# Input casts and side work behind each product's evictions, and another order of the last steps, in a four-layer decoder step

## The chip, the cores and the metric

The kernel runs on one core of one Trainium2 chip. What counts is the time of one execution in microseconds (us). A core has a tensor engine for matmuls (PE; its weight loads are PEld), a vector engine (VectorE, in the profile DVE), a scalar engine (ScalarE, ACT), GpSimd (POOL) and a sync engine (SyncE, SP). SP here does little but start transfers (DMAs) between the memory outside the core and its on-chip buffer. Matmul results land in PSUM, a small memory in banks. ACT and DVE take them out of there, which is called an eviction below. Each engine works through its own list of instructions in order. One that has to wait holds up everything behind it in its list.

## The reference

One step of a decoder: 1,024 prompt positions and 8 single decode positions, width 2,048. There is one pooling layer, then one shared projection to keys and values, then one attention layer with a window of 128. Each layer has an input product, a gate, an output product and a layer norm.

```python
def pool_layer(x, prefix, pos, w_in, w_grp, scale, w_out, g_ln, b_ln):
    z = x @ w_in
    u, gate = z[..., :D_POOL], z[..., D_POOL:]
    d, new_state = multiscale_pool(u, prefix, pos)
    d = jnp.einsum('btgc,gce->btge', d.reshape(B, T, N_POOL_GROUPS, POOL_GROUP), w_grp)
    y = (d.reshape(B, T, D_POOL) * scale * jax.nn.silu(gate)) @ w_out
    return layer_norm(ALPHA * x + y, g_ln, b_ln), new_state

def attn_layer(x, ..., w_in, sinks, w_out, g_ln, b_ln):
    z = x @ w_in
    q = rope_partial(z[..., :D_ATTN].reshape(B, T, N_HEADS, HEAD_DIM), pos)
    gate = z[..., D_ATTN:]
    o = attn_core(q, kb, vb, q_pos, k_pos, sinks).reshape(B, T, D_ATTN)
    y = (o * jax.nn.silu(gate)) @ w_out
    return layer_norm(ALPHA * x + y, g_ln, b_ln)
```

All of it is in fp32.

## The kernel before

**Tiling.** The positions are worked in two chunks of 512 and 520 columns (the second holds the 8 decode positions). Every layer has two phases, its input product (`ai`, `bi`) and its output product (`ao`, `bo`), each over both chunks. A phase computes pairs of output tiles with a Strassen scheme: `seven` makes seven products in place of eight (`ORDER7` is their order: 0, 2, 1, 5, 3, 4, 6). Each product's operands are sums or differences of quarter matrices, and its result is added into the PSUM banks a, b and c in turn (`names`).

**Precision.** A matmul of fp32 is done as three matmuls of rounded operands. Every weight tile and every input tile is split into a rounded high part, which ACT makes by a cast (`cast_to`, L491, for weights; `x_cast`, L796, for inputs), and a residual, which DVE makes by a subtraction (L506 in `prep_to` for weights, L805 in `x_make` for inputs). One product is 8 times the three matmuls L661, L662 and L663.

**A product's steps.** `begin` first calls `flush`, which runs the list `posts`, the evictions of the product before. Then it asks for loads and prepares weights three to seven products ahead. Then `run` issues the 24 matmuls and puts this product's own eviction in `posts`, and `end` follows. The evictions are p0 (L609, ACT), p2 (L615, ACT), p1 (L618, ACT), p5 (L624, ACT), p3 (L629, DVE), p4 (L634, DVE) and p6 (L641, ACT). Since the banks go round, one product later PE wants the bank back that an eviction is reading.

**What stands in `end`.** Sums of weights that come late, products from other work (`self.pe`), the `events` due at this product, and then two things in which the change lies. `x_tick` (L812) looks whether an input tile of the next phase may be loaded, cast (L796) or given its residual (L805); each depends on the free buffers and the tile's age. Below it the side work, generators that make sums of weights (L439 to L444) or a layer norm of the chunk before (L932 to L934, L1005), takes a step if enough buffers are free. `in_order` at the end of the program pins the lists of PE, DVE and ACT to the order in which the source issues them, so nothing is moved later.

**The end.** `phase_end` closes the last layer for the second chunk. `TAIL` is an order of the last products in which three pairs of tiles (x, y, z) are interleaved, and `steps` says which small work goes with which product. Behind the last product the layer norm needs the moments of two halves of the columns (A and Bh). `affine1` (two DVE operations, L1423 and L1424) and `affine2` (two ACT operations, L1431, and a store) scale a pair of tiles. Most rows leave the core transposed: `turn` transposes on PE (L1531), `last_rows` adds a rank-one term (L1540), `factors` transposes the row factors (L1519), `evict` takes 512 columns out of PSUM, on ACT (L1554) or DVE (L1552), and starts a 512 KB store to `y1b` (second half) or `y1a` (first half) for every two. `last_four` (L1565 to L1568 and a store) writes the few columns that are left. `moments` is a chain that goes between ACT and DVE (L1500 to L1512, L1497).

## Time and profile before

| | before |
|---|---|
| runs, us | 2304.54, 2304.70, 2308.23 |
| median, us | 2304.7 |
| the profiled execution, us | 2305.89 |
| its span in the trace, us | 2304.1 |
| granted TensorE clock, mean | 0.999 |
| instructions | 50417 |
| bytes moved by DMA, MB | 654.58 |

The span runs from the first to the last instruction or transfer in the trace; the execution's own time is 1.79 us more. In the rows below, a row of the timeline gives start, duration, engine, line, operation, shapes, and in brackets the idle time ahead of it and what ended it. A row of the windows gives a stretch of time and, for each engine, its busy us and its instructions, then the granted clock, the share of the DMA engines that was busy and GB/s. A matmul of this kernel is started every 0.12 us though each lasts 0.28 us, since matmuls overlap; PE's idle time is therefore read from the brackets.

### The profile page before, as it was taken

The numbers are of one execution on the slowest core, as the hardware profiler recorded it, in microseconds if no ns is written. First come the engines' busy times: TensorE is split into PE (matmuls) and PEld (weight loads), VectorE is DVE, ScalarE is ACT, GpSimd is POOL, SyncE is SP. The second block draws the span as 40 slices with busy tenths as digits, with TensorE's granted clock in tenths as the row PEclk, the third lists the DMA queues.
The fourth block names the chain that finished last, engine by engine and source line by source line (L and its number), as shares of the span: only waits on it lengthen the run. The fifth ranks groups of instructions, "written<-read, shape, count | busy, mean of one in ns | idle before, by whom it ended". The sixth has DMA issues, their size and how long they took to land. (4 is left out here: it accounts for less than half of the span.)

```text
span 2304.1 us, 50417 instructions
## 1 busy us (share of the span) xinstructions
PE 2283.5 (99%) x20279; PEld 2209.6 (96%) x20279; DVE 1902.1 (83%) x2433; ACT 1368.2 (59%) x2533; POOL 198.1 (9%) x400
## 2 busy tenths in 40 slices
PE   9999999999999999999999999999999999999998
PEld 7899999999999999999889999999999999999998
DVE  8787889777878878988888888899776777888896
ACT  4444446544546546555466776785776678656565
POOL 0111110011010000000011111100000000010001
PEclk9999999999999999999999999999999999999999
DMA  8768789988989988999687667787686678799794
GB/s 292 243 233 296 262 298 364 328 306 289 309 306 313 350 286 305 338 389 351 230 305 255 230 231 248 256 291 233 223 255 229 218 225 306 250 364 383 254 347 172
DMA packets 248220, 654.58 MB, mean 284 GB/s; under 512 B 26385, under 2 KB 106033, under 8 KB 247985
## 3 DMA queue, kind: packets, MB, share of 16 engines
q1 hardware_dynamic: 204816, 494.67, 63.8%
q0 software_dynamic: 43168, 156.68, 17.6%
q8 instruction: 159, 2.61, 0.5%
q14 instruction: 77, 0.62, 0.1%
HBM read 464.54 MB, written 177.20 MB: 279 GB/s over the span
## 5 line engine op out<-in xcount | busy, mean ns | idle before, releaser
L661 PE MATMUL pD<-m,m 128*128 128x260 f32 (+1 forms) x4976 | 1409.1, 283 | 6.8 <-DVE m L629 3.0
L662 PE MATMUL pD<-m,m 128*128 128x260 f32 (+1 forms) x4976 | 1401.8, 282 | 0.0
L663 PE MATMUL pD<-m,m 128*128 128x260 f32 (+1 forms) x4976 | 1401.2, 282 | 0.6 <-DVE m L506 0.5
L661 PEld LDWEIGHTS pD<-m,m 128*128 128x128 f32 x4976 | 936.8, 188 | 12.1 <-issue 2.3
L663 PEld LDWEIGHTS pD<-m,m 128*128 128x128 f32 x4976 | 937.3, 188 | 1.1 <-DVE m L506 1.1
L662 PEld LDWEIGHTS pD<-m,m 128*128 128x128 f32 x4976 | 936.8, 188 | 0.5
L506 DVE TENSOR_TENSOR m<-m,m 128x1024 fp32r<-128x1024 f32 x684 | 827.6, 1218 | 76.7 <-ACT m L491 42.9
L491 ACT CAST m<-m 128x1024 fp32r<-128x1024 f32 x684 | 712.8, 1048 | 286.8 <-DVE m L343 86.4
L343 DVE TENSOR_TENSOR m<-m,m 128x1024 f32<-128x1024 f32 x120 | 146.6, 1222 | 10.2 <-DMA m<-in_wia 6.9
L805 DVE TENSOR_TENSOR m<-m,m 128x1024 fp32r<-128x1024 f32 (+1 forms) x118 | 144.2, 1225 | 5.9 <-ACT m L796 3.2
L641 ACT COPY m<-pD 128x260 f32<-128x260 f32 (+1 forms) x87 | 32.5, 374 | 188.5 <-PE pD L663 188.5
L796 ACT CAST m<-m 128x1024 fp32r<-128x1024 f32 (+1 forms) x118 | 123.8, 1054 | 4.4 <-DMA m<-in_x 2.4
L689 PE MATMUL pD<-m,m 128*128 128x512 f32 x288 | 114.3, 397 | 0.0
L691 PE MATMUL pD<-m,m 128*128 128x512 f32 x288 | 113.5, 394 | 0.0
L690 PE MATMUL pD<-m,m 128*128 128x512 f32 x288 | 113.2, 393 | 0.0
L629 DVE TENSOR_TENSOR m<-pD,m 128x260 f32<-128x260 f32 (+1 forms) x90 | 38.1, 423 | 74.9 <-PE pD L663 74.9
L1870 ACT ACTIVATE m<-m,sm 128x128 f32<-128x128 f32 x256 | 99.3, 390 | 0.0
L1892 ACT ACTIVATE m<-m,sm 128x128 f32<-128x128 f32 (+1 forms) x320 | 93.8, 373 | 0.0
L1133 PE MATMUL pD<-m,m 128*128 128x260 f32 (+1 forms) x528 | 91.4, 323 | 0.0
L1133 PEld LDWEIGHTS pD<-m,m 128*128 128x128 f32 x528 | 79.4, 188 | 8.2
L618 ACT COPY m<-pD 128x260 f32<-128x260 f32 (+1 forms) x90 | 33.6, 374 | 90.3 <-PE pD L663 90.2
L609 ACT ACTIVATE pD<-pD 128x260 f32<-128x260 f32 (+1 forms) x88 | 32.5, 369 | 78.2 <-PE pD L663 68.2
(257 smaller groups left out, 2187.4 us busy)
## 6 DMA issues: line engine op xcount, KB each, us to landing
m<-in_wib SPq DMA_DIRECT2D x132, 512.0 KB
m<-in_wia SPq DMA_DIRECT2D x122, 512.0 KB
swia<-m POOLq DMA_DIRECT2D x64, 512.0 KB, 5.0
m<-swia SPq DMA_DIRECT2D x64, 512.0 KB
m<-swoa SPq DMA_DIRECT2D x64, 512.0 KB
m<-swob SPq DMA_DIRECT2D x56, 512.0 KB
m<-in_wob SPq DMA_DIRECT2D x52, 512.0 KB
m<-in_woa SPq DMA_DIRECT2D x48, 512.0 KB
```

Of the source, the lines that this page charges most:

```text
L343: self.nc.vector.tensor_add(s[out].a[:, :1024], s[x].a[:, :1024], s[y].a[:, :1024])
L491: self.nc.scalar.copy(hi.r[:, :1024], self.stream[self.cast].src().a[:, :1024])
L506: self.nc.vector.tensor_sub(lo.r[:, :1024], s.src().a[:, :1024], hi.a[:, :1024])
L661: nc.tensor.matmul(ps[:, :TH], wh[:, s], h, start=new and k == 0, stop=False, skip_group_check=on)
L662: nc.tensor.matmul(ps[:, :TH], wh[:, s], l, start=False, stop=False, skip_group_check=on)
L663: nc.tensor.matmul(ps[:, :TH], wl[:, s], h, start=False, stop=k == 7, skip_group_check=on)
L689: nc.tensor.matmul(ps[:], wh[:, s], h, start=par == 0 and k == 0, stop=False)
L690: nc.tensor.matmul(ps[:], wh[:, s], l, start=False, stop=False)
L691: nc.tensor.matmul(ps[:], wl[:, s], h, start=False, stop=par == 1 and k == 7)
L796: self.nc.scalar.copy(h.r[:, :n], s.a[:, :n])
L805: self.nc.vector.tensor_sub(l.r[:, :n], s.a[:, :n], h.a[:, :n])
L1133: nc.tensor.matmul(ps[:, : cs.stop - cs.start], ws[:, s], d[:, cs], start=f0 and k == 0, stop=l0 and k == 3,)
```

## The change

`end` no longer runs `x_tick` and the side work. It appends both to a new list, `owed`, and `flush` empties that list behind the evictions, at the next `begin` (and in the plain products `unit` and `two_units` also halfway). In the last steps, `affine1(4, Bh)` moves into the step of the product (z, 6); `affine2` can be done by halves, and the half of z goes into `moments` as `early`; a third eviction of the second half goes into `between`, ahead of the cast L1512; `last_four` for the first half stands ahead of the first half's evictions; and the factors and the first `last_rows` stand ahead of transposes.

```diff
--- before.py
+++ after.py
@@ -204,7 +204,7 @@
         self.mem = Mem(pool("mem", bufs=1), NSLOT)
         self.n = 0
         self.i = self.e = self.lastO = self.turns = self.ring = 0
-        self.posts, self.events, self.side = [], {}, []
+        self.posts, self.events, self.side, self.owed = [], {}, [], []
         self.extra, self.on = None, False
         self.fresh = None
         self.ahead = 7, 4, 3
@@ -514,6 +514,8 @@
         todo, self.posts = self.posts, []
         for go in todo:
             go()
+        while self.owed:
+            self.owed.pop(0)()
 
     def begin(self):
         self.flush()
@@ -540,7 +542,9 @@
         for go in self.events.pop(self.i, []):
             go()
         self.i += 1
-        self.x_tick()
+        self.owed += [self.x_tick, self.work]
+
+    def work(self):
         room = len(self.mem.whole()) - 2 * len(self.xq)
         if self.extra and next(self.extra, 1):
             self.extra = None
@@ -1423,13 +1427,14 @@
             nc.vector.tensor_sub(t, t, b2(box["m", h.start]))
             nc.vector.tensor_mul(t, t, b2(box["r", h.start]))
 
-        def affine2(p, h):
+        def affine2(p, h, js=(0, 1)):
             t = tv(p)[:, :, h]
-            for j in range(2):
+            for j in js:
                 m = 2 * p + j
                 g, b = (self.prm[:, i + m : i + m + 1] for i in (gc, bc))
                 nc.scalar.activation(t[:, j], t[:, j], AF.Identity, bias=b, scale=g)
-            nc.sync.dma_start(out[:, 2 * p : 2 * p + 2, :], t)
+            if 1 in js:
+                nc.sync.dma_start(out[:, 2 * p : 2 * p + 2, :], t)
 
         def back(p):
             pre[p] = self.mem.full()
@@ -1486,7 +1491,7 @@
                         skip_group_check=True,
                     )
 
-        def moments(at=0, between=lambda: None):
+        def moments(at=0, between=lambda: None, early=lambda: None):
 
             mb, vb = R[at]
             w, h, S = self.mem.full(), self.mem.full(), [self.mem.half() for _ in range(4)]
@@ -1502,6 +1507,7 @@
             nc.vector.scalar_tensor_tensor(v, vb[:, :TH], EPS, qq, op0=ALU.add, op1=ALU.subtract)
             nc.scalar.mul(X[hi], m[hi, A2], -1.0)
             nc.scalar.copy(M[hi], X[hi])
+            early()
             nc.scalar.activation(r, v, AF.Abs_reciprocal_sqrt)
             back32(32)
             nc.vector.tensor_mul(qq, r, r)
@@ -1606,7 +1612,7 @@
             (z, 5): [
                 lambda: square(y, A), lambda: factors2(TH), lambda: spare(4), lambda: scale(4),
             ],
-            (z, 6): [lambda: add(y, A), lambda: spare(y), lambda: scale(y)],
+            (z, 6): [lambda: add(y, A), lambda: affine1(4, Bh), lambda: spare(y), lambda: scale(y)],
         }
         for p, idx in TAIL:
             for go in steps.get((p, idx), []):
@@ -1643,31 +1649,31 @@
         turn(0, 0, 0, 8)
 
         def between():
-            for b in range(2):
-                evict(B, b, 0)
-
-        moments(0, between)
-        for b in range(2):
-            evict(B, b, 1, "DVE")
-        affine2(z, Bh)
+            evict(B, 0, 0)
+            evict(B, 1, 0)
+            evict(B, 0, 1, "DVE")
+
+        moments(0, between, lambda: affine2(z, Bh, (0,)))
+        evict(B, 1, 1, "DVE")
+        last_four(0, f3, NK, io["y1c"])
         X[0, 0, 2], X[0, 0, 3] = self.psW(), self.psW()
         turn(0, 0, 8, 16)
+        factors(0)
+        factors2(0)
         X[0, 1, 0], X[0, 1, 1] = self.psD(), self.psD()
-        turn(0, 1, 0, 8)
+        turn(0, 1, 0, 4)
+        last_rows(0, 0, range(4))
+        turn(0, 1, 4, 8)
         X[0, 1, 2] = self.psO()
         turn(0, 1, 8, 12)
-        factors(0)
-        factors2(0)
-        affine1(4, Bh)
-        last_rows(0, 0, range(4))
         last_rows(0, 1, range(3))
         for k in range(4):
             evict(0, 0, k)
         X[0, 1, 3] = self.psD()
         turn(0, 1, 12, 16)
         last_rows(0, 1, (3,))
+        affine2(z, Bh, (1,))
         affine2(4, Bh)
-        last_four(0, f3, NK, io["y1c"])
         for k in range(4):
             evict(0, 1, k)
```

The lists of the engines change as follows; the letters m, pD, pO stand for buffers (m on chip, pD and pO in PSUM), and the numbers in them differ between the two kernels. L809, L633, L1291, L1334 and L1560 of the changed kernel are the lines L805, L629, L1287, L1330 and L1554 of the kernel before; L506 keeps its number. L343 sums quarters of a weight, L272 is the residual of a pooled tile, L1287 adds the layer's input to a finished pair of tiles, and L1330 begins the sums of its layer norm.

The first place is DVE's list in the first layer's input product, some 344 us into the program, before the change:

```order
L343 TENSOR_TENSOR m_427_3646<-m_426_3644,m_427_3646 128x1024
L805 TENSOR_TENSOR m_438_3748<-m_416_3593,m_433_3712 128x1040
L629 TENSOR_TENSOR m_434_3714<-pD_3597,m_425_3642 128x256
L506 TENSOR_TENSOR m_440_3753<-m_418_3599,m_437_3720 128x1024
L343 TENSOR_TENSOR m_426_3644<-m_418_3599,m_426_3644 128x1024
```
After:

```order
L343 TENSOR_TENSOR m_427_3646<-m_426_3644,m_427_3646 128x1024
L633 TENSOR_TENSOR m_433_3712<-pD_3597,m_425_3642 128x256
L809 TENSOR_TENSOR m_438_3749<-m_413_3562,m_434_3714 128x1040
L506 TENSOR_TENSOR m_440_3753<-m_420_3603,m_437_3720 128x1024
L343 TENSOR_TENSOR m_426_3644<-m_420_3603,m_426_3644 128x1024
```

Ten rows behind these, still in DVE's list, before:

```order
L506 TENSOR_TENSOR m_447_3828<-m_418_3599,m_445_3794 128x1024
L272 TENSOR_TENSOR m_449_3857<-m_443_3788,m_449_3857 128x512
L805 TENSOR_TENSOR m_450_3860<-m_417_3595,m_439_3750 128x1040
L506 TENSOR_TENSOR m_455_3872<-m_435_3716,m_448_3830 128x1024
L343 TENSOR_TENSOR m_435_3716<-m_435_3716,m_418_3599 128x1024
L805 TENSOR_TENSOR m_457_3903<-m_423_3638,m_451_3862 128x1040
L506 TENSOR_TENSOR m_463_3915<-m_426_3644,m_456_3874 128x1024
```
The same stretch of DVE's list after:

```order
L809 TENSOR_TENSOR m_446_3826<-m_414_3564,m_439_3751 128x1040
L506 TENSOR_TENSOR m_449_3832<-m_420_3603,m_445_3794 128x1024
L272 TENSOR_TENSOR m_451_3861<-m_443_3788,m_451_3861 128x512
L809 TENSOR_TENSOR m_452_3866<-m_418_3599,m_447_3828 128x1040
L506 TENSOR_TENSOR m_457_3876<-m_435_3716,m_450_3834 128x1024
L343 TENSOR_TENSOR m_435_3716<-m_435_3716,m_420_3603 128x1024
L809 TENSOR_TENSOR m_460_3909<-m_419_3601,m_453_3868 128x1040
```

The eviction p3 (the row that reads a pD) has moved ahead of the input residual. Further on, an input residual (L805, now L809) stands ahead of each of three weight residuals (L506) that it stood behind.

The second place is DVE's list in the output product of the same layer, some 910 us in, around the addition L1287 that a pair's evictions end with. Before:

```order
L506 TENSOR_TENSOR m_1273_10787<-m_1250_10640,m_1268_10752 128x1024
L805 TENSOR_TENSOR m_1275_10815<-m_1248_10635,m_1270_10780 128x1040
L1287 SCALAR_TENSOR_TENSOR m_1259_10709<-m_1234_10551,m_1259_10709 128x1024
L506 TENSOR_TENSOR m_1281_10828<-m_1255_10676,m_1274_10789 128x1024
L1330 TENSOR_TENSOR m_1259_10709<-m_1259_10709,m_1111_9436 128x1024
L805 TENSOR_TENSOR m_1283_10859<-m_1249_10637,m_1276_10817 128x1040
L506 TENSOR_TENSOR m_1287_10870<-m_1260_10711,m_1282_10830 128x1024
L805 TENSOR_TENSOR m_1290_10901<-m_1254_10673,m_1284_10861 128x1040
```
After:

```order
L809 TENSOR_TENSOR m_1272_10785<-m_1244_10602,m_1267_10750 128x1040
L506 TENSOR_TENSOR m_1276_10793<-m_1252_10644,m_1271_10758 128x1024
L1291 SCALAR_TENSOR_TENSOR m_1259_10709<-m_1234_10551,m_1259_10709 128x1024
L809 TENSOR_TENSOR m_1278_10823<-m_1250_10640,m_1273_10787 128x1040
L506 TENSOR_TENSOR m_1284_10834<-m_1256_10678,m_1277_10795 128x1024
L1334 TENSOR_TENSOR m_1259_10709<-m_1259_10709,m_1110_9429 128x1024
L809 TENSOR_TENSOR m_1286_10868<-m_1251_10642,m_1279_10825 128x1040
L506 TENSOR_TENSOR m_1290_10876<-m_1263_10717,m_1285_10836 128x1024
L809 TENSOR_TENSOR m_1293_10910<-m_1262_10715,m_1287_10870 128x1040
```

Ahead of L1287 the same number of input residuals has been made in both. Behind it, an input residual now comes first, and each weight residual that follows has one input residual more ahead of it than before.

The third place is ACT's list at the end, from the copy that opens `moments` on. Before:

```order
L1500 COPY m_3008_28269<-pD_28428 128x260
L1503 ACTIVATE m_3013_28488<-m_3008_28269 64x256
L1504 CAST m_3014_28489<-m_3013_28488 64x256
L1505 ACTIVATE m_3016_28491<-m_3015_28490 128x260
L1554 ACTIVATE m_3017_28500<-pD_28454,m_2863_26945 128x512
L1554 ACTIVATE m_3018_28502<-pO_28456,m_2863_26945 128x512
L1512 CAST m_3014_28489<-m_3013_28488 64x256
L1554 ACTIVATE m_3017_28500<-pD_28455,m_2863_26945 128x512
L1554 ACTIVATE m_3018_28502<-pD_28457,m_2863_26945 128x512
L1431 ACTIVATE m_2973_27959<-m_2973_27959,prm 128x260 x2
L1526 COPY m_2863_26945<-pD_28541 128x2
```
After (L1505, L1508, L1509, L1511 and L1518 are L1500, L1503, L1504, L1505 and L1512 of before, and L1435 is L1431):

```order
L1505 COPY m_3009_28270<-pD_28431 128x260
L1508 ACTIVATE m_3014_28491<-m_3009_28270 64x256
L1509 CAST m_3015_28492<-m_3014_28491 64x256
L1435 ACTIVATE m_2973_27946<-m_2973_27946,prm 128x260
L1511 ACTIVATE m_3017_28494<-m_3016_28493 128x260
L1560 ACTIVATE m_3018_28504<-pD_28457,m_2864_26946 128x512
L1560 ACTIVATE m_3019_28506<-pO_28459,m_2864_26946 128x512
L1560 ACTIVATE m_3018_28504<-pD_28458,m_2864_26946 128x512
L1518 CAST m_3015_28492<-m_3014_28491 64x256
L1560 ACTIVATE m_3019_28506<-pD_28460,m_2864_26946 128x512
L1532 COPY m_2864_26946<-pD_28532 128x2
```

One scaling of `affine2` (L1431) has moved ahead of the fourth operation of `moments`, and the third eviction of the second half ahead of the cast L1512; the fourth eviction is behind it as before, and the other scaling has left this stretch.

## The prediction

> **What bounds the kernel now.** The first view is the profile's page, for the busy time of the engines; the second groups PE's idle time by what ended it.
>
> ```profile
> PE 2283.5 (99%) x20279; PEld 2209.6 (96%) x20279; DVE 1902.1 (83%) x2433; ACT 1368.2 (59%) x2533; POOL 198.1 (9%) x400
> ...
> PE pD L661 <- DVE m L629: 3.0, 3, 1.3
> PE pD L661 <- ACT pD L609: 1.7, 2, 1.3
> PE pD L661 <- ACT m L618: 1.5, 1, 1.5
> PE pS L1936 <- DVE m L1903: 1.1, 3, 0.5
> PE pD L663 <- DVE m L506: 0.5, 1, 0.5
> ```
>
> PE is busy for 2283.5 of 2304.1 us, so 20.6 us is all that better order can reach. Work on PE is not changed in number. The rows name who keeps PE waiting: evictions, that is DVE's L629 (3.0 us in 3 waits) and ACT's L609 and L618, and DVE's L1903, a copy of scores. These are the rows that the change can touch; the four hold 7.3 us. For a weight residual, L506, PE waits only once, 0.5 us. The rest is start, end and waits of other kinds. So the forecast is a sum of some ten single waits, and I read each of them in the timeline: does the late eviction stand behind a cast, a residual or side work that the change puts behind it?
>
> **The evictions that come earlier.** Rows of PE give the wait in brackets; rows of DVE and ACT show what the eviction stood behind.
>
> ```profile
> 1237.39 2.35 DVE L805 TENSOR_TENSOR m<-m,m 128x1024 fp32r<-128x1024 f32 x2
> 1240.23 0.36 PE L661 MATMUL pD<-m,m 128*128 128x256 f32 x1 [0.41 <-DVE m L629]
> 1513.71 0.45 PE L1936 MATMUL pS<-m,m 64*64 64x128 f32 x8 [0.26 <-DVE m L1903]
> 1944.98 1.03 ACT L796 CAST m<-m 128x1024 fp32r<-128x1024 f32 x1
> 1945.92 0.36 ACT L609 ACTIVATE pD<-pD 128x256 f32<-128x256 f32 x1
> 1948.01 0.45 PE L1936 MATMUL pS<-m,m 64*64 64x128 f32 x8 [0.49 <-DVE m L1903]
> 2128.76 1.04 ACT L796 CAST m<-m 128x1040 fp32r<-128x1040 f32 x1
> 2130.13 0.39 PE L661 MATMUL pD<-m,m 128*128 128x260 f32 x1 [0.63 <-ACT m L624]
> 2173.68 0.69 DVE L932 TENSOR_TENSOR m<-m 128x512 f32<-128x512 f32 x1 [0.20 <-ACT m L931]
> 2175.74 0.42 DVE L629 TENSOR_TENSOR m<-pD,m 128x260 f32<-128x260 f32 x1
> 2176.31 0.36 PE L661 MATMUL pD<-m,m 128*128 128x260 f32 x1 [1.26 <-DVE m L629]
> ```
>
> In each of the places the row ahead of the eviction is an input residual, an input cast or side work, and lasts longer than PE waits. At 1240, L629 stands behind two residuals of together 2.35 us and PE waits 0.41. At 1948 PE waits for a copy of scores (L1902, which DVE's L1903 reads) that stands behind L609 and the cast L796 of 1.03; the wait at 1513.71 has the same shape. At 2130 it is the cast, 1.04 against a wait of 0.63. At 2176 it is side work: L932 to L934 took from 2173.68 to 2175.74, PE waited 1.26, and in the changed order L629 stands ahead of all three. The sum is 0.41 + 0.26 + 0.49 + 0.63 + 1.26 = **3.05 us**, each term taken whole because the work that is put behind is longer than the wait. What is late next: the cast, the residual or the layer norm that was put behind. A cast or residual is made for a tile that some later product reads, and the layer norm for an output, so a delay of 0.4 us is covered by the products between. If that cover were gone, the term would return as a wait for the moved work, up to the eviction's own 0.36 to 0.42.
>
> **Two stretches in which DVE has no room.** The first is the input product of the first layer.
>
> ```profile
> 344.26 1.22 DVE L343 TENSOR_TENSOR m<-m,m 128x1024 f32<-128x1024 f32 x1 [1.47 <-DMA m<-in_wia]
> 345.40 1.23 DVE L805 TENSOR_TENSOR m<-m,m 128x1040 fp32r<-128x1040 f32 x1
> 346.56 0.42 DVE L629 TENSOR_TENSOR m<-pD,m 128x256 f32<-128x256 f32 x1
> 347.12 0.36 PE L661 MATMUL pD<-m,m 128*128 128x256 f32 x1 [1.29 <-DVE m L629]
> 356.16 1.05 ACT L796 CAST m<-m 128x1040 fp32r<-128x1040 f32 x1
> 357.12 0.36 ACT L609 ACTIVATE pD<-pD 128x256 f32<-128x256 f32 x1
> 357.54 0.38 PE L661 MATMUL pD<-m,m 128*128 128x256 f32 x1 [1.27 <-ACT pD L609]
> ...
> 343.00:372.00 29.00, 26.30 (x217) 25.71 (x217) 27.53 (x31) 18.62 (x24) 2.13 (x4) 1.00 0.91 315
> ```
>
> Taken alone, both waits would nearly go: L629 stands 1.16 behind L805 (345.40 to 346.56), L609 0.96 behind L796, of 1.29 and 1.27 waited, together 2.12 us. But the row of the window gives DVE 27.53 busy of 29.00: it idles 1.47, all of it in the wait for a load at 344.26. The work of DVE in this stretch does not shrink, and by the order some ten rows on one input residual more stands ahead of each of three weight residuals, 1.16 us for one (345.40 to 346.56). So DVE itself allows 1.47 - 1.16 = 0.3 us of gain, and only where the load that it waits for comes earlier by that. The bounds are +2.1 us, where those weight residuals have time to spare, and -1.2 us, where the load comes when it came and PE then waits for a weight residual by the whole step. I take **+0.3 us**, since the window row is nearest to the question.
>
> The second stretch is the output product of that layer.
>
> ```profile
> 912.92 1.23 DVE L1287 SCALAR_TENSOR_TENSOR m<-m,m 128x1024 f32<-128x1024 f32 x1 [1.30 <-ACT m L641]
> ...
> 929.10 0.39 PE L663 MATMUL pD<-m,m 128*128 128x260 f32 x1 [0.51 <-DVE m L506]
> 935.43 0.50 PE L910 MATMUL pO<-m,jr 128*128 128x512 f32 x1 [0.35 <-DVE m L894]
> ...
> 908.00:938.00 30.00, 29.15 (x239) 28.57 (x239) 28.70 (x28) 23.38 (x33) 0.54 (x1) 1.00 0.98 364
> ```
>
> DVE is busy 28.70 of 30.00 and its only pause is the 1.30 ahead of L1287, which waits for the pair's last eviction. Before, a weight residual comes first behind L1287. In the changed order an input residual stands directly behind L1287 and ahead of the weight residuals, so each is late by the step of 1.16 us until the counts are equal again just ahead of L894. PE already waits 0.51 for one of them at 929.10, so that one has no room at all: its wait grows by 1.1 us. L894 is not later, so a PE that comes later no longer waits 0.35 there. Net loss 1.1 - 0.35 = **0.75 us**, with bounds of 0 and 1.2.
>
> **What stays.** The longest wait, 1.52 us for L618 (its row in the groups above), comes from an ACT that a weight cast holds up, and the cast waits for rotary work that counts as an event; events stay ahead of evictions. I put it and the waits of its kind at zero, with 0.5 us either way for chance. The main part then gives 3.05 + 0.3 - 0.75 = **2.6 us**.
>
> **The end.** Behind PE's last matmul the transfers set the end; the row with x24 is a piece of the chain that ended last, the last row one of the windows.
>
> ```profile
> 2283.96 0.43 DVE L639 TENSOR_TENSOR m<-pD,m 128x260 f32<-128x260 f32 x1 [1.23 <-PE pD L663]
> 2284.30 0.69 DVE L1423 TENSOR_TENSOR m<-m,m 128x520 f32<-128x520 f32 x1
> 2284.45 0.59 POOL L1447 COPY m<-m 128x8 f32<-128x8 f32 x1 [3.15 <-DVE m L639]
> 2288.75 0.42 ACT L1505 ACTIVATE m<-m 128x260 f32<-128x260 f32 x1 [0.75 <-DVE m L1502]
> 2290.03 0.68 ACT L1554 ACTIVATE m<-pO,m 128x512 f32<-128x512 f32 x1
> 2291.05 0.40 ACT L1512 CAST m<-m 64x256 fp32r<-64x256 f32 x1 [0.34 <-DVE m L1511]
> 2291.48 1.26 ACT L1554 ACTIVATE m<-pD,m 128x512 f32<-128x512 f32 x2
> 2290.11 2.76 PE pD L1531 x24
> 2292.19 0.92 SPq L1556 DMA_DIRECT2D out_y1b<-m  x2
> 2294.93 0.99 SPq L1556 DMA_DIRECT2D out_y1a<-m  x2
> 2293.00:2302.50 9.50, 2.85 (x17) 2.16 (x15) 3.91 (x9) 4.18 (x9) 0.00 (x0) 0.85 1.01 390
> ```
>
> From 2293.0 to 2302.5 the DMA share is 1.01 at 390 GB/s, 9.5 x 390 = 3.7 MB, which is six stores of 0.52 MB, two of 0.27 (128 x 520 floats) and small ones. So what counts is when the first store starts and whether the queue runs dry. The third eviction, which completes the first store, moves from 2291.48 to directly behind 2290.03 + 0.6: the first store is issued some 0.85 earlier, at 2291.3. But the fourth still needs L1512, so the two y1b stores (2 x 0.52 MB, 2.7 us at 390 GB/s) end near 2294.85, and the stores of y1a must follow. Ahead of the first half's evictions 8 transposes less stand on PE (2.76 us for 24 of them, so 0.9 us for these), but the factors want the bank that the fourth eviction frees, near 2292.3, so I take half, 0.6 earlier than 2294.93, and data some 0.85 behind the issue, as from 2292.19 to where the window of transfers begins: 2295.2. The queue is dry for 0.3. From there 2.63 MB at 390 GB/s take 6.7, to 2301.9 instead of 2302.5: **0.6 us**, bounds 0.2 (the queue runs dry longer) and 0.9 (not at all). The scaling of 0.69 + 0.70 goes into VectorE's pause of 1.23 and makes L639 late by 0.15, which DVE passes to `moments`; ACT's wait of 0.75 ahead of L1505 takes up the scaling that is put there, at half of that wait or all of it, and neither is seen by the first store, which waits for L1554.
>
> L1423 at 2284.30 lasts 0.69 although a copy on POOL runs beside it (2284.45, 0.59): DVE's next instruction was not held up by it. [...]
>
> **The sum.** 2.6 + 0.6 = 3.2 us. From the profiled execution's 2305.89 that gives 2302.7; this execution was 1.2 us above the median of the three runs, so on the median it is 2304.7 - 3.2 = **2301.5 us**.
>
> **The rivals.**
>
> *All of it goes.* The weight residuals have time to spare in both stretches: 3.05 + 2.1 + 0.9 = 6.1 us, with nothing lost, **2298.6 us**. For it: most weight residuals are made three products ahead, and DVE idles 17% over the span. Against it: the two windows, where DVE is 95% busy.
>
> *It is taken up again.* Casts and residuals come later throughout, and another of these tight places takes what an eviction gave; only the end gains: 2304.7 - 0.6 = **2304.1 us**. For it: waits move along a full engine rather than vanish. Against it: in 1200 to 2200 us DVE has pauses ahead of most evictions, where lateness ends.
>
> *Slower.* In the changed order input residuals stand ahead of weight residuals that they stood behind, and PE needs the weight residuals first. Each place where a weight residual has no room costs 1.16 us. I count one such place, behind 912, and half of one behind 344; with three more the kernel would be slower than before, and with eight it would be so by 8 x 1.16 - 3.2 = 6.1 us, **2310.8 us**. For it: L805's work is the same 1.23 us wherever it stands, and the ticks are moved in every phase. Against it: before, PE waits for a weight residual only once, so most have room for a step.
>
> *It doesn't do what it says.* The order shows evictions ahead of the ticks on both engines, so this has no chance left.
>
> **How the numbers follow.** Chances: forecast 0.45, all of it 0.22, taken up again 0.23, slower 0.10. A measurement of this kernel can tell 0.2%, 4.6 us, from no change, so faster means below 2300.1 and slower above 2309.3. All of the second case and a fifth of the first are faster: 0.22 + 0.09 = 0.31. Of the last case 0.08 is slower. The rest, 0.61, is within. The range begins 0.6 below the second case's time, at 2298.0, since the waits held at zero may move by 0.5 too, and ends 1.2 above the third's, for one more tight place, at 2305.3; outside lie the last case and a tenth of the others.
>
> **What would show it.** Right: no waits of PE for L629, L609 or L624 behind a tick at 1240, 2130 and 2176; the waits for L1903 gone at 1513 and 1948; a wait for L506 near 929 of about 1.6; the first y1b store near 2291.3 of the old time scale. Wrong: PE's idle total not below 18, new waits for L506 or L805 in other stretches, loads that come later because buffers come free later, or a hole of over 0.5 us in the transfers of the last ten.

## The result and the profile after

The changed kernel is slower, by 0.8%.

| | before | after |
|---|---|---|
| median of the runs | 2304.7 us | 2323.9 us |
| lowest and highest | 2304.5 to 2308.2 (3 runs shown above) | 2322.5 to 2326.0 (6 runs) |
| ratio, 95% interval | | 1.0079 (1.0069 to 1.0090) |
| profiled execution | 2305.89, span 2304.1 | 2325.30, span 2323.4 |
| PE busy / idle within the span | 2283.5 / 20.6 | 2292.8 / 30.6 |

One more run of the kernel before, taken beside these, lasted 4520.59 us; nothing on record says why, and neither the table nor the ratio counts it.

The forecast was 2301.5, its range 2298.0 to 2305.3: the time lies 22.4 us above the one and 18.6 above the upper end of the other. The span grew by 19.3 us, half of it idle time of PE (+10.0), half busy time of PE (+9.3), although PE does the same work.

In the changed kernel four lines have been added ahead of the matmuls, so L661 is now L665, L663 is L667, the first eviction of a product, L609, is L613, L618 is L622, L629 is L633, L639 is L643, the input cast L796 is L800, the residual L805 is L809, the store L857 is L861, L1903 is L1909. The weight cast and the weight residual keep L491 and L506. The first view is the page of the changed kernel (busy time), the second its list of waits of PE: line that waited, line waited for, us in total, times, longest.

```profile
PE 2292.8 (99%) x20279; PEld 2217.1 (95%) x20279; DVE 1902.3 (82%) x2433; ACT 1367.9 (59%) x2533; POOL 196.6 (8%) x400
...
PE pD L665 <- ACT pD L613: 11.8, 4, 4.9
PE pD L667 <- DVE m L506: 2.6, 6, 0.6
PE pD L665 <- ACT m L622: 2.1, 1, 2.1
PE pD L1525 <- ACT m L1560: 1.5, 1, 1.5
PE pD L2252 <- POOL m L1056: 1.3, 1, 1.3
PE pS L1942 <- DVE m L1909: 1.1, 3, 0.5
```

The row for DVE's L629 (now L633), 3.0 us before, is gone, and so is that for ACT's L624: this is what the change was forecast to do. In its place ACT's L613, the first eviction of a product, has gone from 1.7 us in 2 waits to 11.8 in 4. The four are single rows of PE's timeline:

```profile
356.99 0.38 PE L665 MATMUL pD<-m,m 128*128 128x256 f32 x1 [2.43 <-ACT pD L613]
1064.43 0.39 PE L665 MATMUL pD<-m,m 128*128 128x260 f32 x1 [1.07 <-ACT pD L613]
1284.20 0.39 PE L665 MATMUL pD<-m,m 128*128 128x256 f32 x1 [3.33 <-ACT pD L613]
1502.64 0.58 PE L665 MATMUL pD<-m,m 128*128 128x256 f32 x1 [4.93 <-ACT pD L613]
```

**Why L613 is late.** ACT's timeline ahead of three of these rows:

```profile
355.10 1.04 ACT L491 CAST m<-m 128x1024 fp32r<-128x1024 f32 x1 [2.71 <-DVE m L809]
356.05 0.61 ACT L271 CAST m<-m 128x512 fp32r<-128x512 f32 x1
356.57 0.36 ACT L613 ACTIVATE pD<-pD 128x256 f32<-128x256 f32 x1
...
1281.19 1.04 ACT L491 CAST m<-m 128x1024 fp32r<-128x1024 f32 x1 [4.70 <-DMA to<-m]
1282.14 0.20 ACT L1874 ACTIVATE sm<-sm 128x8 f32<-128x8 f32 x1
...
1283.79 0.36 ACT L613 ACTIVATE pD<-pD 128x256 f32<-128x256 f32 x1
...
1499.62 1.04 ACT L491 CAST m<-m 128x1024 fp32r<-128x1024 f32 x1 [7.17 <-DMA to<-m]
```

The weight cast L491 waits 4.70 and 7.17 us for a DMA named `to<-m`. That is not a load: it is a store, by which a tile leaves for the scratch array `to` in HBM. The cast doesn't read what the store carries. It writes into the buffer that the store is still reading, and begins when the store has landed (the stores at 1281.17 and 1499.46, the casts at 1281.19 and 1499.62). The names in the order of the changed kernel (buffer, then a running number of the allocation) say so, on POOL and on ACT:

```
230 L861 DMA to0_87<-m42_1732_14784 128x1024
...
923 L491 CAST m42_1739_14839<-m20_1726_14661 128x1024
```

Buffer m42 is given to a stored tile as allocation 1732, and the weight cast takes the same buffer as allocation 1739, seven later. At the second place it is m39 (allocations 1952 and 1960). At 355.10 the cast writes the buffer from which DVE's L809 has just read an input tile. In the kernel before, no cast stands so close behind a store: the shortest distances there are 10, to an eviction copy and to a load, and 11, one of them to a weight cast. The chain that ended last runs through both stores (start, duration, line):

```profile
1275.40 5.77 DMA to<-m
...
1490.53 8.93 DMA to<-m
```

So the change put input casts, residuals and side work between the evictions and the weight cast of the next product; these take the buffers that stood free, and the weight cast gets the one that has just been released. (Whether another rule of handing out could have spared these two casts no run shows; `e5_other_buffers`, below, is the nearest.) The eviction L613 stands behind the cast in ACT's list and runs behind it (1283.79 and 1281.19 above), and PE waits for it until 1284.20.

**Why PE is busier.** The windows behind three of the waits (busy time of PE, PEld, DVE, ACT, POOL, then the granted clock, DMA share, GB/s):

```profile
358.00:360.00 2.00, 2.00 (x11) 2.00 (x11) 1.97 (x3) 1.12 (x2) 0.00 (x0) 0.50 1.08 381
1286.00:1289.00 3.00, 3.00 (x16) 3.00 (x16) 2.59 (x4) 2.34 (x8) 0.00 (x0) 0.50 0.46 188
1502.00:1507.00 5.00, 4.36 (x20) 4.37 (x21) 3.44 (x5) 4.30 (x14) 0.53 (x1) 0.50 1.08 327
```

After the long waits, near 1502 already during it, the TensorE clock is granted at 0.50, three times for 3.4 us and once, near 1502, for 6.8, and matmuls follow each other by 0.21 us instead of 0.12. Each matmul of the main stream was compared with its counterpart before: the lag grows behind the four drops (near 357, 1284, 1502 and 1589) by 1.5, 1.6, 2.3 and 1.5 us, which is 6.9 of the 9.3 us of added busy time.

**The account.** The same comparison gives where the lag came and went (us, after minus before, at the program's places): 347 -1.5; 357 to 360 +2.6; 931 to 936 -0.6; 962 to 1005 +2.6; 1060 +1.3; 1240 -0.6; 1272 to 1282 +5.0; 1488 to 1505 +7.8; 1572 to 1580 +2.1; 2130 -0.9; 2169 to 2176 -1.5; 2281 +0.9. The last matmul of the products begins 17.3 us later (2300.98 instead of 2283.64), and from there to the end of the span it takes 22.4 instead of 20.5, another +1.9.

### The profile page after: what moved, and what is told of

It reads as the page before. It is cut to its first block, busy times and chain, and to the rows that moved or that the text cites. A ratio compares the mean times of both kernels' runs of the same rounds, so it can differ in the third digit from the quotient of the medians.

```text
span 2323.4 us, 50388 instructions
## 1 busy us (share of the span) xinstructions
PE 2292.8 (99%) x20279; PEld 2217.1 (95%) x20279; DVE 1902.3 (82%) x2433; ACT 1367.9 (59%) x2533; POOL 196.6 (8%) x400
## 5 line engine op out<-in xcount | busy, mean ns | idle before, releaser
L665 PE MATMUL pD<-m,m 128*128 128x260 f32 (+1 forms) x4976 | 1413.0, 284 | 13.9 <-ACT pD L613 11.8
L667 PE MATMUL pD<-m,m 128*128 128x260 f32 (+1 forms) x4976 | 1405.7, 282 | 2.8 <-DVE m L506 2.6
L665 PEld LDWEIGHTS pD<-m,m 128*128 128x128 f32 x4976 | 940.3, 189 | 19.2 <-ACT pD L613 12.6
L667 PEld LDWEIGHTS pD<-m,m 128*128 128x128 f32 x4976 | 940.9, 189 | 4.5 <-DVE m L506 4.4
L506 DVE TENSOR_TENSOR m<-m,m 128x1024 fp32r<-128x1024 f32 x684 | 828.1, 1219 | 89.1 <-ACT m L491 49.3
L491 ACT CAST m<-m 128x1024 fp32r<-128x1024 f32 x684 | 711.8, 1048 | 306.3 <-DVE m L343 81.2
L343 DVE TENSOR_TENSOR m<-m,m 128x1024 f32<-128x1024 f32 x120 | 146.6, 1222 | 7.6 <-DMA m<-in_wia 4.0
L809 DVE TENSOR_TENSOR m<-m,m 128x1024 fp32r<-128x1024 f32 (+1 forms) x118 | 144.3, 1226 | 8.5 <-ACT m L800 4.4
L800 ACT CAST m<-m 128x1024 fp32r<-128x1024 f32 (+1 forms) x118 | 123.9, 1054 | 4.1 <-DMA m<-in_x 2.6
L633 DVE TENSOR_TENSOR m<-pD,m 128x260 f32<-128x260 f32 (+1 forms) x90 | 38.0, 423 | 85.0 <-PE pD L667 84.8
L622 ACT COPY m<-pD 128x260 f32<-128x260 f32 (+1 forms) x90 | 33.7, 374 | 85.6 <-PE pD L667 85.5
L613 ACT ACTIVATE pD<-pD 128x260 f32<-128x260 f32 (+1 forms) x88 | 32.4, 368 | 74.8 <-PE pD L667 63.7
```

What stands on the lines that cost most here:

```text
L343: self.nc.vector.tensor_add(s[out].a[:, :1024], s[x].a[:, :1024], s[y].a[:, :1024])
L491: self.nc.scalar.copy(hi.r[:, :1024], self.stream[self.cast].src().a[:, :1024])
L506: self.nc.vector.tensor_sub(lo.r[:, :1024], s.src().a[:, :1024], hi.a[:, :1024])
L665: nc.tensor.matmul(ps[:, :TH], wh[:, s], h, start=new and k == 0, stop=False, skip_group_check=on)
L667: nc.tensor.matmul(ps[:, :TH], wl[:, s], h, start=False, stop=k == 7, skip_group_check=on)
L800: self.nc.scalar.copy(h.r[:, :n], s.a[:, :n])
```

## The experiments

The theory: side work and casts, by the place at which they now stand, take buffers and leave the weight cast one that is still in use; the lower clock behind the wait adds to it (1.5 to 2.3 us a time, as above). The rival: the order itself holds back evictions or weight residuals by engine time. All ratios are against runs of the kernel before on the same chip.

**Either half of the moved work alone.** In `e1_tick_ahead` the input ticks run at the end of a product as before, and only side work is put behind the evictions; in `e2_work_ahead` it is the other way round. The end is the new one in both.

```diff
-        self.owed += [self.x_tick, self.work]
+        self.x_tick()
+        self.owed.append(self.work)
```

> The changed kernel with one half undone: x_tick runs at the end of a product again, ahead of the evictions; only the side work is behind them, and the last steps are in their new order. Theory (buffers): the loss comes from weight casts (L491) that are given an on-chip buffer whose store is still running, so that ACT waits and the eviction p0 behind the cast is late. In this kernel's order the cast near 1281 us still gets the buffer of the store to 'to' 7 allocations behind it, the cast near 1499 does not (11 allocations, and a residual). So the wait of PE for p0 near 1284 (3.3 us, and some 1.1 more at a lower clock) stays, the one near 1503 (4.9 us and 2.3 at the lower clock) goes, and those near 357 and 1064 go: about 2311 us. Rival (order): the loss comes from casts and residuals that stand behind evictions and are late for PE; then with the ticks ahead nearly all of it goes: about 2303 us.

Measured 2312.44 us, ratio 1.0028 (1.0017 to 1.0040). The wait at 357 is as before (1.29), those near 1284 and 1502 are 1.48 and none; the loss from 962 to 1005 is there as in the changed kernel (2.7 us). The cast near 1281 waits for the store, as its 7 allocations had named, but 2.19 us where it was 4.70, since the store takes 3.3 us from issue to landing here and 5.8 there; no lower clock follows. So the time fits the theory better than the wait does, for which it expected 3.3.

> The other half undone: the side work runs at the end of a product again, ahead of the evictions; only x_tick is behind them, and the last steps are in their new order. Theory (buffers): in this kernel's order the cast near 1499 us gets the buffer of a running store 8 allocations behind it, the cast near 1281 does not (10 allocations, and an eviction copy). So PE waits near 1503 for p0 (about 5 us, and 2 more at the lower clock), not near 1284; the waits near 357, 930 to 1005 and 1064 stay, if they come from the ticks: about 2315 us. Rival (order): the ticks hold nearly the whole loss: about 2322 us.

Measured 2319.23, ratio 1.0059 (1.0047 to 1.0072). The wait at 357 is there (2.43), the one of 3.33 near 1284 is not; 3.57 near 1492, where the cast waits 5.82 for its store (8 allocations), and a new one of 3.08 near 1604, which nothing had named; no loss from 962 to 1005. So the wait at 357 comes with the ticks and the loss at 962 to 1005 with side work. The long ones behind 1200 belong to neither alone: each variant draws its own, since each hands out the buffers in its own sequence.

**The two parts of the diff.** `e3_owed_alone` has the new order of ticks and side work with the old end, `e4_end_alone` the reverse.

> The kernel before with the list of owed ticks and side work alone; the last steps are in their old order. From the last matmul of the products to the end of the span the changed kernel takes 22.4 us, the one before 20.5. Theory: that comes from side work which ends later, so that its stores stand ahead of the loads of the last tiles and the moments chain starts 3.7 us later; it is the owed list's doing, not that of the new order of the last steps, and this kernel takes as long as the changed one or a little longer: 2324 us. Rival: the new order costs the 2 us (PE waits 1.5 us for a bank at L1525): then 2322 us.

Measured 2323.58, ratio 1.0077 (1.0063 to 1.0090), with the waits of the changed kernel (2.44, 1.07, 3.21 and 4.77 us).

> The kernel before with the new order of the last steps alone; ticks and side work are ahead of the evictions as before. Theory (as predicted): the end is shorter by 0.6 us, 2304.1 us, the main part is unchanged. Rival: the wait of 1.5 us of PE at L1525 makes the end longer by up to 2 us: 2306.7 us.

Measured 2306.29, ratio 1.0001 (0.9992 to 1.0010). The whole loss is the owed list's; the new end by itself is worth nothing that can be measured, in either direction. (The interval reaches from 1.8 us of gain to 2.3 of loss, so the forecast 0.6 is neither seen nor excluded.)

**Other buffers, same rules of order.** In `e5_other_buffers` a buffer that has been stored counts as released 40 releases later rather than 10, so that others go first.

```diff
-        self.mem.release(self, 10 if stored else 0)
+        self.mem.release(self, 40 if stored else 0)
```

> The changed kernel with one number changed: a buffer whose content is still being stored counts as freed 40 releases later instead of 10, so it is given out later. DVE's and ACT's lists stay the same up to some 1200 us and differ little behind it. By this kernel's order the cast near 1281 us no longer gets the buffer of the store to 'to'; the cast near 1499 still does, 8 allocations behind the store, since no other is free; a cast near 1255 now gets one 5 behind a store. Theory (buffers): PE's wait for p0 near 1284 (3.3 us and 1.1 at the lower clock) goes, the one near 1503 (4.9 and 2.3) stays, a small one may come near 1255: 2319 to 2321 us. Rival (order): both stay: 2324 us.

Measured 2364.32, ratio 1.0249 (1.0235 to 1.0263): a miss for both. The cast near 1281 now waits 5.07 us for another store (`th<-m`), and the one near 1514 still waits 4.28 for `to<-m`, with 2.05 of PE behind it. In all there are ten waits for L613 (16.8 us) and nine for weight residuals (6.5). One number in the rule by which the 54 buffers are handed out cost 40 us. Up to 1186 us the rows of ACT and DVE keep their order, and there the wait at 357 falls from 2.43 to 0.40 while one of 3.76 comes up at 1008: with the order the same, only the buffers can have moved these. Behind 1186 some rows move as well, so the rest of the 40 us is not the buffers' alone. That speaks for buffers as the cause of such waits, and against this remedy.

**The phases with the long waits as before.** In `e8_not_in_attention` the changed kernel runs ticks and side work at the end of a product, as before, in the two input projections of the second block alone (`bi0`, `bi1`).

```diff
-        self.owed += [self.x_tick, self.work]
+        if self.ph[:2] == "bi":
+            self.x_tick()
+            self.work()
+        else:
+            self.owed += [self.x_tick, self.work]
```

> The changed kernel, but in the phases of the attention layer's input product (bi) ticks and side work run ahead of the evictions as before; the other phases and the end are as changed. By the order no weight cast gets a buffer less than 11 allocations behind its store. Theory (buffers): the waits near 1284 and 1503 go (12 us with the clock), also the 2 us of growth at 1575; what stays is 4 us up to 1064 and 2 us at the end, less 1.5 us gained at 2130 and 2176: 2309 us. Rival (order, in all phases): the loss spreads over the other phases: 2318 us or more.

Measured 2310.86, ratio 1.0025 (1.0015 to 1.0034): a hit. The waits of 3.33 and 4.93 us are gone with the half clock behind them; those at 357 (2.44) and 1060 remain, and the gains of 2130 to 2176 too.

**More of the suspected cost.** In `e11_side_work_later` the changed kernel starts side work only with two more buffers free.

```diff
-        room = len(self.mem.whole()) - 2 * len(self.xq)
+        room = len(self.mem.whole()) - 2 * len(self.xq) - 2
```

By its order six weight casts in `bi0` and `bi1`, rather than two, get a buffer whose store was issued 5 to 8 allocations earlier. That is a count read ahead of the run.

> The changed kernel with side work that starts only when two more buffers are free; DVE, ACT and PE get the same work. By the order five more of the casts that stand right ahead of the softmax (L491 ahead of L1874) now get the buffer of a store that is 5 or 6 allocations old, six in all with the one 8 behind its store; the changed kernel has two. Theory (buffers): PE waits for p0 at each of them, 3 to 5 us and 1 to 2 at the lower clock, so four more than before between 1284 and 1503: 2340 to 2352 us. Rival (order): side work that runs a little later changes nothing much: 2320 to 2326 us.

Measured 2390.44, ratio 1.0374 (1.0358 to 1.0390). PE's timeline has six waits for L613 in that stretch, the six that the order names:

```profile
1285.83 0.39 PE L665 MATMUL pD<-m,m 128*128 128x256 f32 x1 [3.32 <-ACT pD L613]
1363.84 0.39 PE L665 MATMUL pD<-m,m 128*128 128x256 f32 x1 [3.27 <-ACT pD L613]
1422.97 0.58 PE L665 MATMUL pD<-m,m 128*128 128x256 f32 x1 [4.18 <-ACT pD L613]
1480.12 0.39 PE L665 MATMUL pD<-m,m 128*128 128x256 f32 x1 [3.50 <-ACT pD L613]
1518.75 0.58 PE L665 MATMUL pD<-m,m 128*128 128x256 f32 x1 [8.58 <-ACT pD L613]
1549.85 0.58 PE L665 MATMUL pD<-m,m 128*128 128x256 f32 x1 [5.43 <-ACT pD L613]
```

The size was above the expectation, since each wait drew others behind it (four of 2.4 us for L628) and one of 10.3 us came at the end. ACT's casts ahead of these six wait for a store each, 4.25, 5.51, 6.46, 5.71, 9.73 and 7.67 us, five times for `to<-m` and once for `th<-m`. The count is what the theory had named and the rival had not. Together with `e8`, where the two places vanish with their cause, I take the stores as shown for the two long waits.

**Weights first.** If the new order is bad because it takes buffers ahead of the weight cast, the owed work can be put behind the next product's weight cast and residual as well. `e6_behind_weights` does so in all phases (the list is emptied after the weights are prepared, not in `flush`), with the old end; `e7_behind_weights_end` is the same with the new end.

> Ticks and side work not between the evictions and the weights' casts and residuals, but behind both (at the end of begin instead of the end of flush); the last steps in their old order. By the order no weight cast gets a buffer less than 14 allocations behind its store (7 and 8 in the changed kernel), and every weight residual stands ahead of the input residual of the same step. Theory (buffers, and weight residuals that are late behind input residuals): the long waits for p0 go, those for L506 too, and the earlier evictions keep what they gave (1.5 us at 347, 0.8 at 936, 0.4 at 1240, 0.7 at 2130, 1.4 at 2176): 2300 to 2302 us. Rival (order: casts and residuals of input tiles come too late): more waits of PE for L805's line and the ticks' casts: above 2305 us.

Measured 2373.04, ratio 1.0292 (1.0278 to 1.0306): a miss, though half of the theory is in it. Up to 936 this kernel is 5.3 us ahead of the kernel before, with both waits at 347 and 357 gone; behind 1000 it loses step by step, and from 2032 to 2090 it waits up to 10.7 us at a time for weight residuals, which is a row of its list of waits:

```profile
PE pD L667 <- DVE m L506: 30.5, 6, 10.7
```

Which step starves them wasn't traced.

> The same with the new order of the last steps. If DVE has its pause ahead of the last eviction again, the new end costs nothing and gains up to 0.6 us: the time of the kernel above, less 0 to 0.6. Rival: the new end costs 1 us, as the profiles with and without it show when DVE is late.

Measured 2372.76, ratio 1.0289 (1.0274 to 1.0303): the new end changes nothing here either.

`e9_weights_first_early` keeps the gain and drops the rest: owed work behind the weights in the first block's input projections and its first output projection, all else as before, with the old end; `e10_weights_first_early_end` adds the new end. `e12_two_places` adds to `e9` the changed order (behind evictions) in the last output projection (`bo1`), up to where the kernel's end begins. The piece of the edit of `e9` that chooses the phases:

```diff
-        self.x_tick()
+        if self.ph in ("ai0", "ai1", "ao0"):
+            self.owed += [self.x_tick, self.work]
+        else:
+            self.x_tick()
+            self.work()
```

> Ticks and side work behind the evictions and behind the weights' casts and residuals, but only in the first layer's input product and the first chunk of its output product (to some 980 us); from there on, and at the end, all as in the kernel before. Theory: where buffers are free, the earlier evictions and weight residuals give what the run with this order in all phases showed up to 936 us, 5.2 us, and nothing is lost behind: 2300 us. Rival: what is gained is lost again behind 980 us, since the input tiles of the next phases are made later (that run lost 1.8 us near 1010, 2.0 near 1065 and 4.4 near 1221): 2305 us or more.

> The same with the new order of the last steps. With an undisturbed stream ahead of it the new end showed no difference that could be measured (1.0001, 0.9992 to 1.001): the time of the kernel above within 1 us. Rival: it gains 0.6 us by its earlier first store.

> Owed list as in e9_weights_first_early, and used once more where the second output projection ends (until the last phase's end), where the changed kernel gained 0.65 us at 2130 and 1.4 us at 2169 to 2176 and no cast had to wait for a store. Theory (the gains are of the order alone, and stay where the buffers in front of the stream are not the ones just stored): e9's gains of about 2 us at the last product's matmul grow by 1.5 to 2 us, time 2301.5 to 2302.5. Rival (what is gained late is given back at the end, or the buffers fall otherwise): 2303.5 to 2305, as e9.

| | us | ratio, 95% interval |
|---|---|---|
| `e9_weights_first_early` | 2303.84 | 0.9993 (0.9984 to 1.0002) |
| `e10_weights_first_early_end` | 2304.51 | 0.9995 (0.9987 to 1.0004) |
| `e12_two_places` | 2302.71 | 0.9992 (0.9983 to 1.0001) |

In the trace of `e9` the stream is 3.4 us ahead at 357 and 2.1 at its end, in that of `e12` 3.6 and 4.7, with gains of 0.6 at 2130 and 1.5 at 2176, where the changed kernel had 0.9 and 1.5; the list of waits of PE in `e12` has neither an L629 (here L640) above 0.3 nor a weight residual above 0.5:

```profile
PE pD L672 <- ACT m L629: 1.5, 1, 1.5
PE pD L2262 <- POOL m L1067: 1.3, 1, 1.3
PE pS L1952 <- DVE m L1919: 1.1, 3, 0.5
PE pD L674 <- DVE m L507: 0.9, 2, 0.5
...
PE pD L672 <- DVE m L640: 0.3, 1, 0.3
```

(L629 is here what L618 was before: the wait that was held at zero, unchanged.) So the gains that the prediction had read are there and add up where the buffers stay out of it, but the three intervals all reach 1.000: none of these beats the kernel before by more than the measurement can tell, and the times of `e9` and `e12` fall between what their theories and their rivals expected. `e10` takes as long as `e9`, as expected.

## Why the prediction was wrong

**The step that failed** is the sentence on what is late next: "A cast or residual is made for a tile that some later product reads, and the layer norm for an output, so a delay of 0.4 us is covered by the products between." It follows the moved work to its readers and not to its buffers. A cast, a residual and a side-work tile each take a buffer when they are issued, and by moving the issue ahead of the next weight cast they took the one which that cast would have got. The prediction named "loads that come later because buffers come free later" as a sign of being wrong and gave it no term. It was the largest: 11.8 us of waits for L613 where 1.7 had been, 6.9 of clock behind waits, against a forecast gain of 3.2. The two waits of 3.33 and 4.93 with their clock are shown to be stores by `e8` and `e11`, the one at 357 to hang on the buffer by `e5`; the one of 1.07 at 1064 is not shown. Nor is why the wait for L622 at 1589 grew from 1.52 to 2.12 and so drew 1.5 of the 6.9.

**The rival that came nearest** was the one that ends slower, by another mechanism: weight residuals ahead of which input residuals stand, 1.16 us at a place. PE's waits for L506 did grow, from 0.5 us once to 2.6 in six, none over 0.6. That is a ninth of the loss.

**The single waits at 1240, 2130 and 2176** were right in place and about in size: the stream gained 0.6, 0.9 and 1.5 there for waits of 0.41, 0.63 and 1.26. How much such a wait differs from one execution to the next shows in `e4`, whose rows of ACT and DVE are those of the kernel before in order up to 2283: there PE waits 1.21 at 1240, 1.42 at 2130 and 1.26 at 2176. Two of the three are 0.8 us from the trace that the prediction was read from, so that the sizes came out so near is in part luck.

**The waits for L1903 at 1513 and 1948** were mis-read. They stayed, 1.1 us in three, because the input cast didn't go behind the eviction for good. ACT in the changed kernel, just ahead of the place at 1948 (now 1966):

```profile
1959.66 0.38 ACT L645 COPY m<-pD 128x260 f32<-128x260 f32 x1 [3.00 <-PE pD L667]
1960.07 1.08 ACT L2002 ACTIVATE m<-m 128x1040 f32<-128x1040 f32 x1
1961.05 1.03 ACT L800 CAST m<-m 128x1024 fp32r<-128x1024 f32 x1
1961.98 1.04 ACT L491 CAST m<-m 128x1024 fp32r<-128x1024 f32 x1
...
1964.58 0.36 ACT L613 ACTIVATE pD<-pD 128x256 f32<-128x256 f32 x1
1964.88 1.00 ACT L1908 COPY m<-pS 128x1024 f32<-128x1024 f32 x1
```

The cast that stood directly ahead of L609 (1944.98) is put behind, but the one of the product ahead has moved into the same stretch, ahead of the softmax rows. ACT has as much to do ahead of L613 as it had, and 1964.58 is 1945.92 plus the lag there. "Each term taken whole because the work that is put behind is longer than the wait" needed an engine with a pause; ACT had none between 1960 and 1965.

**The stretch 344 to 372**: forecast +0.3 with bounds +2.1 and -1.2; measured 1.5 gained at 347 and 2.6 lost at 357 to 360, net -1.0, inside the bounds. The loss was not the weight residual but the buffer above. `e9`, with the weights first, gains 3.4 here, more than the upper bound, so what the window's 1.47 us of idle DVE seemed to forbid was possible. (Nor was all of that idle time the wait for the load: the wait of 1.47 begins 0.2 us ahead of the window.)

**The stretch 908 to 938**: forecast a loss of 0.75 with L506's wait near 929 at 1.6; measured 0.47 and a net gain of 0.7. In `e8`, with the same order here, that wait is 1.25 and the net loss 0.1, since 0.6 comes back at 936. In `e4`, with the order of before, it is 0.94 where it had been 0.51. The growth of 1.1 was 0.7 in one run and absent in another, and no run shows the net loss. The loss of 2.6 from 962 to 1005, of which waits for L506 hold 1.5, wasn't forecast; by `e1` and `e2` it belongs to side work, and its step is still open. That the cast at 1063 is late because its load waits for a buffer is likewise only argued.

**The end**: forecast 0.6 gained; 1.9 lost in this trace, and by the times of `e4` nothing by itself. The scaling was put into VectorE's pause of 1.23, and in the changed kernel there was no pause:

```profile
2301.28 0.69 DVE L1410 TENSOR_TENSOR m<-m,m 128x520 f32<-128x520 f32 x1
2301.89 0.69 DVE L1427 TENSOR_TENSOR m<-m,m 128x520 f32<-128x520 f32 x1
2302.62 0.70 DVE L1428 TENSOR_TENSOR m<-m,m 128x520 f32<-128x520 f32 x1
2303.24 0.42 DVE L643 TENSOR_TENSOR m<-pD,m 128x260 f32<-128x260 f32 x1
...
2311.49 0.44 PE L1525 MATMUL pD<-cst,m 128*128 128x128 f32 x2 [1.54 <-ACT m L1560]
```

Against the last matmul (2300.98; 2283.64 before) L643 begins 2.3 us behind it instead of 0.3. Without the two scaling rows it could have begun where L1410 ends, 1.0 behind: the scaling adds 1.3, not the 0.15 forecast, and 0.7 comes from a DVE that was late already. The first store of `y1b` is issued 9.2 us behind the last matmul; 7.7 was forecast and 8.55 had been.

Where the stream is not disturbed, the forecast held up to that store and not beyond it. In `e4` that eviction (there L644) begins 0.34 behind the last matmul (2284.51), where it had been 0.32, and the first store of `y1b` is issued 7.7 behind. But the first store of `y1a` is issued 11.1 behind, where it had been 11.3: 0.2 earlier, not 0.6. The wait of the factors for a bank, which was to leave half of the 0.9, is 0.62 in `e4` and 1.54 in the changed kernel (half of 0.9 is 0.45 besides, not the 0.6 that was taken). So the queue runs nearly dry: from 2295.5 to 2296.4 it moves 107 GB/s in `e4`, and the hole is some 0.9 where 0.3 was forecast. Three pairs of traces differ in the end alone (`e4` and before, `e10` and `e9`, the changed kernel and `e3`); from the last matmul to the end of the span the new order takes 1.0, 0.8 and 1.0 us longer in them, in single executions. The run times don't resolve that.

VectorE was not held up by the copy on GpSimd beside it, as the row of L1423 had said: L1427 takes 0.69 at 2303.57 with the copy beside it and 0.69 at 2301.89 without one. The copy began 0.15 behind L1427, ended 0.06 behind it and took 0.60, where the copy at 2300.48 took 0.19. Why it took longer no run shows. A row of each engine from the changed kernel's end:

```profile
2303.57 0.69 DVE L1427 TENSOR_TENSOR m<-m,m 128x520 f32<-128x520 f32 x1
2303.72 0.60 POOL L1452 COPY m<-m 128x8 f32<-128x8 f32 x1 [3.04 <-DVE m L643]
```

## What to carry to other kernels

Where on-chip buffers are handed out in program order, moving an instruction moves an allocation: before pricing a new order, follow for every moved instruction which buffer it takes and who gets the next one, above all whether an in-order engine that something urgent stands behind will write a buffer that a store is still reading. Count the distance from each stored tile to the next user of its buffer in both orders; here 7 and 8 allocations ahead of two casts cost 12 us with the half clock behind them, and in the kernel before 10 and more cost PE nothing. The count finds the places and doesn't price them: the cast with 7 cost PE 1.48 us in `e1`, and a weight residual with 7 in the changed kernel stands still for 2.93 us until its store has landed at 1256.7, and PE doesn't wait there. And an instruction that is moved behind an eviction stands ahead of the next one: it gains where the engine has a pause between the two, and gained nothing here where ACT had none (1960 to 1965; PE's waits for L1909 stayed, 1.1 us in three).

## What the runs showed of the hardware

In these traces a lower clock followed the longer waits of PE, and not from a sharp bound on. Over the traces of the changed kernel and of `e1`, `e2`, `e6`, `e8` and `e11`, waits within the stream up to 1.7 us were never followed by a lower clock, waits of 3.0 us and more always were (0.50 within two us of PE's resuming, or already during the wait), and of 13 waits between 2.0 and 2.5 us nine were, four not. In `e5`, waits of 1.46 (at 2331.95), 1.64 (at 2035.38) and 1.93 (at 1073.61) were followed by 0.50 as well, and others of 1.64 to 2.10 weren't. The wait at 357, 2.43 us long in the changed kernel and in `e2`, was followed by 0.50 in the one and by 1.00 in the other; at 1284 the drop began 1.5 us after PE had resumed. In `e6` a wait of 2.04 was followed by 0.50 once. What sets when the clock drops, no run shows. Each of the four drops in the changed kernel cost 1.5 to 2.3 us beside its wait, so the wait of 3.33 us cost nearly 5.

A store of a 128x1024 tile (0.5 MB) held its buffer for 5.8 and 8.9 us in the chain of the changed kernel, and the cast that wanted the buffer waited 4.70 and 7.17 of these. In `e1` the cast at the same place waited 2.19.
